# A transformer layer on one core: where the softmax sums are finished, in which order six and two merged tiles enter the output projection, and when LN1's statistics are called

## The chip, the cores and the metric

The kernel runs on one core of one Trainium2 chip. The metric is device time in microseconds of one execution; the median of several runs counts. An execution's span, from its first to its last instruction in the profile, is a little shorter than its device time.

Engines go by their short names: PE is TensorE, DVE VectorE, ACT ScalarE, POOL GpSimd, SP SyncE. Each engine takes its instructions in a fixed order and waits at one whose inputs are not ready or whose output buffer is still in use.

## What is computed

One layer of a diffusion backbone: 1024 latent tokens and 256 context tokens of width 1024. Two attention branches in parallel, A with a window of 128 to either side and a sink logit for each head, B over all keys; both also see the context keys. Eight heads each, 64 wide, two groups of keys and values. The branches are merged by sigmoid gates and projected; then come a residual with LayerNorm (LN1), a SwiGLU feed-forward with a convolution, and LN2. Cut to what matters here:

```python
def _sink_softmax(scores, sink):
    sink = sink.astype(jnp.float32)[:, :, None, None]
    m = jnp.maximum(jnp.max(scores, axis=-1, keepdims=True), sink)
    e = jnp.exp(scores - m)
    return e / (jnp.sum(e, axis=-1, keepdims=True) + jnp.exp(sink - m))

def _merge_branches(o_a, o_b, gate_logits, w_branch_a, w_branch_b, w_out):
    g_a, g_b = jnp.split(jax.nn.sigmoid(gate_logits), 2, axis=-1)
    return (g_a * (o_a @ w_branch_a) + g_b * (o_b @ w_branch_b)) @ w_out
...
        h = x * (1.0 + scale1) + shift1
        y = _latent_token_mixer(h, kv_ctx, w_in[l], b_in[l], attn_sink[l], q_norm_g[l], k_norm_g[l],
                                w_branch_a[l], w_branch_b[l], w_out[l], rope)
        x = _layer_norm(DEEPNORM_ALPHA * x + gate1 * y, ln1_g[l], ln1_b[l])

        h = x * (1.0 + scale2) + shift2
        y = _conv_ffn(h, w_up[l], conv_w[l], conv_b[l], w_down[l])
        x = _layer_norm(DEEPNORM_ALPHA * x + gate2 * y, ln2_g[l], ln2_b[l])
```

Branch B uses the ordinary softmax.

## The kernel before

All data are float32. For a product a value is split into a rounded high part and the rest (`split`, L86 the cast on ACT, L88 that on POOL, L91 the subtraction), and three matmuls make one product: high by high (L94), high by low (L95), low by high (L96), in `mm3`.

**Attention.** There are 32 units (class `Unit`, L421): branch A first, then B, eight blocks of 128 queries each, two groups of four heads each. The loop over u interleaves three lists by fractional positions: the score steps of unit u, the value steps of unit u-1, and other work that fills in (projections of the branches). Inside this stage a scheduler sets the order on every engine from the order in which the code issues and from its own estimates; the code's order is not the final one.

- Score steps: `context` (in B: four passes over the context keys, matmuls into `s_x`, then `cxp` at L515 on DVE, which writes `p_x`), four times `lat` (L466: matmuls L451/L452 into `s`, a pass on DVE at L497 that scales and finds the maximum, the exponential on ACT at L464 with the sum into `sm`, in B also the context's sum into `smc`), then `norm`, and the preparation of a later unit's queries (`qtr`).
- `norm` finishes the softmax sums of a unit. In A it adds the maximum and the sink (L522), takes the exponential on ACT (L523, tile `f`) and adds it to `sm` (L524); in B it adds `smc` to `sm` (L524). Then comes the reciprocal (L525). All of these are 128x4.
- Value steps: `tr_step` transposes four 128x128 pieces of probabilities on PE (L562) into `ptr`; ACT casts them to `pth` (L571) and DVE subtracts to get `ptl` (L572), or POOL does it for some key blocks; `av_step` multiplies by the values (L583 with `pth`, L584 with `ptl`). A step is one key block in A and two in B. `rows`, inserted as the third value step, transposes the reciprocal sums (L529, `str`), copies them and sends them through DRAM to all partitions (`rb`); the unit's last step, `out_step`, multiplies by `rb` on POOL (L598).
- `ptr`, `qtr` and `str` share three buffers in PSUM; `s` has two.

**Output projection.** `merge(f)` (L997) adds the two branches' gated results for the f-th of eight tiles (DVE, L999) and splits the sum into `mh` (ACT) and `ml` (DVE). `half(f, hf)` makes the product of branch B that `merge(f)` needs. `y_pair(f, s)` (L1252) makes the output tiles f and f+1 for the tokens in s: for each, eight merged tiles k by three matmuls of 128x512, with the weights `hwo` and `lwo`. From L1264 on the order of PE is the one written in the code.

**Planner.** `mm_ticked` (L1229) calls `tick` (L1086) after each k, which advances a counter by 640 for 512 columns. Steps in `pend` are issued when the counter reaches their number; the first step of LN1's first half (512 tokens) is `stats`, and its number is the first of `LN1_F` (L38), counted from the first k of `y_pair` over the second half's tokens. `stats` (L1106) issues 16 matmuls 128x1 (L1113 of `zs`, L1114 of `zq`) and a few small instructions on DVE and POOL; `diags` and `cast` (L1130) follow, then the tiles' normalization, which makes the operands of the up projection. `zs` and `zq` are the sums over tiles of the residual and of its square, added up on POOL (L1080) and DVE (L1081) as the tiles of `y` are done.

Of the kernel before, what the change touches and what calls it, by code (L numbers as in the profile page):

```python
# [9 lines left out]
AF = mybir.ActivationFunctionType  # L10
ALU = mybir.AluOpType
AX = mybir.AxisListType

P = 128
# [3 lines left out]
KT = 8  # L18
# [10 lines left out]
HALF = 512  # L29
# [5 lines left out]
FILL_END = 26  # L35
XPOS = 2
SPAN = 0.8, 0.85
LN1_F = 3500.0, 5100.0, 100.0  # L38
LN1_D = (2500.0, 2000.0, 2000.0, 2500.0), (300.0, 3700.0, 300.0, 500.0), (100.0, 1000.0, 300.0, 500.0)
LN2_D = 4000.0, 2800.0, 2000.0, 1200.0, 1300.0  # L40
LN2_E = 3500.0, 1500.0, 1500.0, 500.0, 400.0
# [30 lines left out]
def layer_kernel(  # L72
# [6 lines left out]
    nc = tc.nc  # L79
# [13 lines left out]
    def mm3(ps, a, b, start, stop, resumed=False):  # L93
        nc.tensor.matmul(ps, a[0], b[0], start=start, stop=False, skip_group_check=resumed)  # L94
        nc.tensor.matmul(ps, a[0], b[1], start=False, stop=False, skip_group_check=resumed)  # L95
        return nc.tensor.matmul(ps, a[1], b[0], start=False, stop=stop, skip_group_check=resumed).ins  # L96
# [12 lines left out]
    sinkb = ctile([P, 8], F32, "sinkb")  # L109
# [125 lines left out]
    for n in (0, 1):  # L235
        s = slice(n * HALF, (n + 1) * HALF)
# [10 lines left out]
    w = modulate(0)  # L247
    for k in range(KT):
# [5 lines left out]
        for t in range(NT):  # L254
            s = slice(t * P, (t + 1) * P)
            mm3(acc[t], (hT[k][0][:, s], hT[k][1][:, s]), w, k == 0, k == KT - 1)
        w = wn
# [163 lines left out]
    class Unit:  # L421
# [82 lines left out]
        def cxp(self):  # L504
# [7 lines left out]
            for h in range(4):  # L512
# [2 lines left out]
                nc.vector.tensor_scalar(out=p[:, c], in0=s[:, c], scalar1=self.qscale(nqs)[:, h:h + 1], scalar2=TOP,  # L515
                                        op0=ALU.mult, op1=ALU.min, accum_out=self.other[:, h:h + 1])

        def norm(self):
            hc = slice(self.g * 4, self.g * 4 + 4)
            more = self.smc if self.br else small(f"f_{self.id}", (P, 4))  # L520
            if not self.br:
                nc.vector.tensor_tensor(out=more, in0=self.nm, in1=sinkb[:, hc], op=ALU.add)  # L522
                nc.scalar.activation(more, more, AF.Exp)  # L523
            nc.vector.tensor_tensor(out=self.sm, in0=self.sm, in1=more, op=ALU.add)  # L524
            nc.vector.reciprocal(self.sm, self.sm)  # L525

        def rows(self):
# [11 lines left out]

        def score_steps(self):  # L540
            steps = [lambda h=h: self.lat(h) for h in range(4)]
            return steps + [self.norm]

        def context(self):
            self.begin()
# [8 lines left out]
        def value_steps(self):  # L554
# [57 lines left out]
            self.av_step, self.out_step = av_step, out_step  # L612
            g = 1 + self.br
            steps = [lambda n=n: step(range(n, n + g)) for n in range(0, len(kt), g)]
            steps.insert(2, self.rows)
            return steps

    tokens = []
# [125 lines left out]
    steps = [(gi, k, a) for gi, k in order for a in ((0, 1) if gi == "g" else (0,))]  # L744
# [15 lines left out]
    for n, (gi, k, a) in enumerate(steps):  # L760
# [17 lines left out]
        w = ready.pop((gi, k, 0))  # L778
        c = ready.pop(("c", k), None)
        for t in tiles:  # L780
            if t < NT:
                s = slice(t * P, (t + 1) * P)
                x = hT[k][0][:, s], hT[k][1][:, s]
            else:
                s = slice((t - NT) * P, (t - NT + 1) * P)
# [45 lines left out]
    def small(name, shape):  # L831
        return att.tile(list(shape), F32, tag=name.split("_")[0], name=name,
                        bufs=4)
# [58 lines left out]
    for u in range(nu + 1):  # L892
# [8 lines left out]
        if u == 29:  # L901
            first = branch_steps(1, w_b, (0, 1), att, (nc.gpsimd, nc.gpsimd), (0,),
                                 lambda: [ht(f"{a}wb1_0", (P, 8, P), R32) for a in "hl"])
# [74 lines left out]
    mrg = []  # L978
# [6 lines left out]
    wts = {}  # L985
# [45 lines left out]
    for f in range(2, KT):  # L1031
# [3 lines left out]
        ps = pb[f]  # L1035
# [190 lines left out]
        a, n = {"T3": ("13", 0), "T1": ("13", 1), "T4": ("24", 0), "T2": ("24", 1)}[name]  # L1226
        return tp[a + "h", k][:, n], tp[a + "l", k][:, n]

    def mm_ticked(o, w, a, s, n=KT):  # L1229
        for k in range(n):  # L1230
            mm3(o, (w[0][:, k], w[1][:, k]), (a[k][0][:, s], a[k][1][:, s]), k == 0, k == n - 1)
            tick((s.stop - s.start) / 0.8)

    npair = [0]
# [17 lines left out]
    def y_pair(f, s, first=False):  # L1252
        w = s.stop - s.start
        ps = big(f"y{f}_{s.start}_{w}")
        for a in (0, 1):
            mm_ticked(ps[:, a * HALF:a * HALF + w], wts[f + a], mrg, s)
        for a in (0, 1):
            wout_z(f + a, s, ps[:, a * HALF:a * HALF + w], first and a == 0)

# [14 lines left out]
    for f in (4, 6):  # L1274
        for si in (1, 2):
# [3 lines left out]
            elif f == 6:  # L1279
                second = ln1(2)  # L1280
                a = [n for n in range(len(pend)) if len(pend) - n <= KT]
# [122 lines left out]
    for k in range(4):  # L1404
        steps = build(k)
# [245 lines left out]
    s = LN2_S[-1]  # L1651
# [181 lines left out]
```

## Time and profile before

| | us |
|---|---|
| median of three runs | 1550.84 |
| the three runs | 1550.83, 1550.84, 1552.32 |
| the profiled execution | 1552.42 |
| its span | 1550.6 |
| PE busy | 1526.3 |
| DVE busy | 1164.9 |
| ACT busy | 802.1 |
| POOL busy | 753.1 |

The profile is of one execution, with a mean granted clock of 0.997. Matmuls overlap in it: the row of a matmul lasts longer than the step to the next one, so a stall of PE is read from start to start. In a row of the timeline stand start, duration, engine, line, operation, output and inputs, shapes, and in square brackets how long the engine was idle before it and what ended that. Attention lies between about 320 and 780 us, the output projection between 794 and about 890, the feed-forward behind it.

### The profile page before, as it was taken

To read this page: it belongs to the slowest core of one execution; us is meant where nothing else is said; L and a number is where in the kernel's file an instruction comes from. 1 tells how busy PE (TensorE), PEld (TensorE's weight loads), DVE (VectorE), ACT (ScalarE), POOL (GpSimd) and SP (SyncE) were. 2 spreads that over 40 slices of the span, in tenths; PEclk is the share of its full clock that TensorE was granted. 3 is DMA by queue.
4 is the path that set the end of the run, shared out by engine and by line. 5 is a ranking of instruction groups with operands and counts; after the bars stand their busy time and mean duration, and the time that the engine had idled before them with its cause. 6 is when DMAs were issued, how large, how long until landed. Compare 5 with 4: busy or idle time off the path is not lost. (4 is left out here: it accounts for less than half of the span.)

```text
span 1550.6 us, 21959 instructions
## 1 busy us (share of the span) xinstructions
PE 1526.3 (98%) x7652; PEld 1269.6 (82%) x7652; DVE 1164.9 (75%) x1783; ACT 802.1 (52%) x1420; POOL 753.1 (49%) x697
## 2 busy tenths in 40 slices
PE   9999999999999999999999999999999999999997
PEld 7888888878887788888778988888888888888886
DVE  7588847538888667788565879888888887657796
ACT  5422223448888666788422664544444444435542
POOL 0374303426666466565423555766666675021063
PEclk9999999999999999999999999999999999999999
DMA  9667663322236555543451223233334446996732
GB/s 379 244 214 260 234 227 91 112 88 63 63 106 163 133 120 130 116 93 86 161 146 59 82 82 109 95 111 114 115 109 105 113 109 174 368 276 214 256 113 91
DMA packets 111873, 229.73 MB, mean 148 GB/s; under 512 B 13489, under 2 KB 27313, under 8 KB 111666
## 3 DMA queue, kind: packets, MB, share of 16 engines
q1 hardware_dynamic: 96464, 199.20, 38.4%
q0 software_dynamic: 10400, 20.19, 8.5%
q10 hardware_dynamic: 4898, 8.94, 1.5%
q8 instruction: 60, 0.98, 0.3%
q14 instruction: 51, 0.42, 0.1%
HBM read 177.09 MB, written 65.87 MB: 157 GB/s over the span
## 5 line engine op out<-in xcount | busy, mean ns | idle before, releaser
L572 DVE TENSOR_TENSOR ptl<-ptr,pth 128x512 fp32r<-128x512 f32 x188 | 123.5, 685 | 32.6 <-ACT pth L571 31.8
L91 DVE TENSOR_TENSOR ld<-rd,hd 128x1024 fp32r<-128x1024 f32 x77 | 96.6, 1271 | 49.8 <-ACT hd L86 47.7
L562 PE MATMUL ptr<-ident,p 128*128 128x128 f32 x816 | 127.0, 277 | 5.5 <-DVE ptl L572 2.7
L571 ACT CAST pth<-ptr 128x512 fp32r<-128x512 f32 x188 | 105.5, 586 | 50.6 <-PE ptr L562 35.6
L464 ACT ACTIVATE p<-p,nm 128x1024 f32<-128x1024 f32 (+2 forms) x128 | 125.1, 979 | 10.5 <-DVE p L497 10.0
L86 ACT CAST hd<-rd 128x1024 fp32r<-128x1024 f32 x77 | 79.6, 1051 | 85.6 <-PE p L96 56.3
L562 PEld LDWEIGHTS ptr<-ident,p 128*128 128x128 f32 x816 | 95.1, 140 | 33.4 <-DVE ptl L572 7.7
L583 PE MATMUL av<-pth,VT 128*128 128x512 f32 x236 | 105.0, 445 | 1.2 <-ACT pth L571 0.9
L94 PE MATMUL p<-hd 128*128 128x512 f32 x264 | 103.2, 391 | 0.0
L96 PE MATMUL p<-hd,ld 128*128 128x512 f32 x264 | 102.7, 389 | 0.0
L95 PE MATMUL p<-ld,hd 128*128 128x512 f32 x264 | 102.7, 389 | 0.0
L96 PE MATMUL g<-hh,wlg 128*128 128x512 f32 x256 | 99.7, 390 | 0.4 <-POOL wlg L91 0.4
L94 PE MATMUL g<-hh,whg 128*128 128x512 f32 x256 | 99.9, 390 | 0.0
L95 PE MATMUL g<-hl,whg 128*128 128x512 f32 x256 | 99.6, 389 | 0.0
L584 PE MATMUL av<-ptl,VT 128*128 128x512 f32 x236 | 97.6, 414 | 0.5 <-POOL ptl L91 0.5
L91 POOL TENSOR_TENSOR wlg<-wg,whg 128x512 fp32r<-128x512 f32 x32 | 45.3, 1421 | 99.0 <-ACT whg L86 94.0
L497 DVE TENSOR_SCALAR_CACHE_REDUCE p<-s,cvt,nmc 128x1024 f32<-128x1024 f32 x64 | 84.6, 1339 | 7.4 <-PE ptr L562 5.5
L451 PE MATMUL s<-KL,q 128*128 128x512 f32 (+2 forms) x192 | 77.0, 401 | 1.3 <-DVE p_x L515 1.1
L88 POOL TENSOR_SCALAR pth<-prw 128x512 fp32r<-128x512 f32 x48 | 30.5, 635 | 93.4 <-PE av L583 43.9
L452 PE MATMUL s<-KL,q 128*128 128x512 f32 (+2 forms) x192 | 71.4, 372 | 0.0
L86 ACT CAST wS<-s 128x512 fp32r<-128x512 f32 x76 | 45.2, 620 | 49.7 <-POOL s L1166 48.9
L86 ACT CAST wA<-ru 128x512 fp32r<-128x512 f32 x57 | 35.5, 623 | 61.3 <-PE d L96 32.8
(403 smaller groups left out, 4918.4 us busy)
## 6 DMA issues: line engine op xcount, KB each, us to landing
wml<-in_wmodT_dram SPq DMA_DIRECT2D x48, 512.0 KB
ru<-in_w_up_dram SPq DMA_DIRECT2D x38, 512.0 KB
rd<-td SPq DMA_DIRECT2D x55, 256.0 KB
rd<-sd SPq DMA_DIRECT2D x44, 256.0 KB
rd<-in_w_dn_dram SPq DMA_DIRECT2D x33, 256.0 KB
wm<-in_wmodT_dram SPq DMA_DIRECT2D x16, 512.0 KB
wg<-in_w_g_dram SPq DMA_DIRECT2D x32, 256.0 KB
sgd<-sg ACTq DMA_DIRECT2D x32, 256.0 KB
```

The costliest lines, as they stand in the source:

```text
L86: cast[:] = [nc.scalar.copy(hi, src).ins]
L91: low[:] = [lo_eng.tensor_tensor(out=lo, in0=src, in1=hi.bitcast(F32), op=ALU.subtract).ins]
L94: nc.tensor.matmul(ps, a[0], b[0], start=start, stop=False, skip_group_check=resumed)
L95: nc.tensor.matmul(ps, a[0], b[1], start=False, stop=False, skip_group_check=resumed)
L96: return nc.tensor.matmul(ps, a[1], b[0], start=False, stop=stop, skip_group_check=resumed).ins
L464: nc.scalar.activation(p, s, AF.Exp, bias=nm[:, h:h + 1], scale=scale, accum_out=sm[:, h:h + 1])
L497: nc.vector.tensor_scalar(out=p, in0=o, scalar1=self.qscale(nqs)[:, hs] if self.br else -1.0, scalar2=self.other[:, hs], op0=ALU.mult, op1 ...
L562: nc.tensor.transpose(tr[:, h * P:(h + 1) * P], self.pslice(h, n), ident)
L571: nc.scalar.copy(hi, tr)
L572: nc.vector.tensor_tensor(out=lo, in0=tr, in1=hi.bitcast(F32), op=ALU.subtract)
L583: nc.tensor.matmul(self.av, v, hi, start=first, stop=False)
L584: nc.tensor.matmul(self.av, v, lo, start=False, stop=self.left == 0)
```

## The change

Three edits.

```diff
--- before.py
+++ after.py
@@ -35,7 +35,7 @@
 FILL_END = 26
 XPOS = 2
 SPAN = 0.8, 0.85
-LN1_F = 3500.0, 5100.0, 100.0
+LN1_F = 4500.0, 5100.0, 100.0
 LN1_D = (2500.0, 2000.0, 2000.0, 2500.0), (300.0, 3700.0, 300.0, 500.0), (100.0, 1000.0, 300.0, 500.0)
 LN2_D = 4000.0, 2800.0, 2000.0, 1200.0, 1300.0
 LN2_E = 3500.0, 1500.0, 1500.0, 500.0, 400.0
@@ -515,13 +515,13 @@
                 nc.vector.tensor_scalar(out=p[:, c], in0=s[:, c], scalar1=self.qscale(nqs)[:, h:h + 1], scalar2=TOP,
                                         op0=ALU.mult, op1=ALU.min, accum_out=self.other[:, h:h + 1])
 
+        def sink(self):
+            self.smc = small(f"f_{self.id}", (P, 4))
+            nc.vector.tensor_tensor(out=self.smc, in0=self.nm, in1=sinkb[:, self.g * 4:self.g * 4 + 4], op=ALU.add)
+            nc.scalar.activation(self.smc, self.smc, AF.Exp)
+
         def norm(self):
-            hc = slice(self.g * 4, self.g * 4 + 4)
-            more = self.smc if self.br else small(f"f_{self.id}", (P, 4))
-            if not self.br:
-                nc.vector.tensor_tensor(out=more, in0=self.nm, in1=sinkb[:, hc], op=ALU.add)
-                nc.scalar.activation(more, more, AF.Exp)
-            nc.vector.tensor_tensor(out=self.sm, in0=self.sm, in1=more, op=ALU.add)
+            nc.vector.tensor_tensor(out=self.sm, in0=self.sm, in1=self.smc, op=ALU.add)
             nc.vector.reciprocal(self.sm, self.sm)
 
         def rows(self):
@@ -539,7 +539,7 @@
 
         def score_steps(self):
             steps = [lambda h=h: self.lat(h) for h in range(4)]
-            return steps + [self.norm]
+            return steps if self.br else steps + [self.sink]
 
         def context(self):
             self.begin()
@@ -612,7 +612,8 @@
             self.av_step, self.out_step = av_step, out_step
             g = 1 + self.br
             steps = [lambda n=n: step(range(n, n + g)) for n in range(0, len(kt), g)]
-            steps.insert(2, self.rows)
+            steps[2:2] = [self.rows]
+            steps[1:1] = [self.norm]
             return steps
 
     tokens = []
@@ -1226,9 +1227,9 @@
         a, n = {"T3": ("13", 0), "T1": ("13", 1), "T4": ("24", 0), "T2": ("24", 1)}[name]
         return tp[a + "h", k][:, n], tp[a + "l", k][:, n]
 
-    def mm_ticked(o, w, a, s, n=KT):
-        for k in range(n):
-            mm3(o, (w[0][:, k], w[1][:, k]), (a[k][0][:, s], a[k][1][:, s]), k == 0, k == n - 1)
+    def mm_ticked(o, w, a, s, ks):
+        for k in ks:
+            mm3(o, (w[0][:, k], w[1][:, k]), (a[k][0][:, s], a[k][1][:, s]), k == 0, k == KT - 1)
             tick((s.stop - s.start) / 0.8)
 
     npair = [0]
@@ -1252,8 +1253,9 @@
     def y_pair(f, s, first=False):
         w = s.stop - s.start
         ps = big(f"y{f}_{s.start}_{w}")
-        for a in (0, 1):
-            mm_ticked(ps[:, a * HALF:a * HALF + w], wts[f + a], mrg, s)
+        for ks in (range(6), range(6, KT)) if first and s.start == 0 else (range(KT),):
+            for a in (0, 1):
+                mm_ticked(ps[:, a * HALF:a * HALF + w], wts[f + a], mrg, s, ks)
         for a in (0, 1):
             wout_z(f + a, s, ps[:, a * HALF:a * HALF + w], first and a == 0)
```

**Softmax sums.** `norm` is cut in two. The sink's part, an add on DVE and the exponential on ACT, stays among the score steps of branch A, as `sink`; B has one score step fewer, so the others move in their fractional positions. The add to `sm` and the reciprocal become the second of the unit's value steps, which run in the next iteration: first transposes, `norm`, second transposes, `rows`, and so on. No instruction is added or removed.

**Output projection.** The first `y_pair` (tiles 0 and 1, first half of the tokens) takes k from 0 to 5 for tile 0, then for tile 1, then k 6 and 7 for tile 0 and for tile 1. The other pairs are as before. `tick` is called as often.

**Statistics.** The first number of `LN1_F` goes from 3500 to 4500: with 640 for each k, `stats` is issued after the eighth k instead of the sixth, so after 24 matmuls of 128x512 instead of 18. What follows counts from there.

The following rows show the instructions in an engine's order. A name ends in a number of the buffer, which differs between the two kernels and means nothing.

PE at the beginning of the output projection, before (`y0_0_512` is the pair's result; `mh5`, `ml5` the sixth merged tile, `hwo0`, `lwo0` the weights of output tile 0):

```order
L96 MATMUL y0_0_512_8997<-mh5_8866,lwo0_8873 128x512
L94 MATMUL y0_0_512_8997<-mh6_8911,hwo0_8872 128x512
L95 MATMUL y0_0_512_8997<-ml6_8912,hwo0_8872 128x512
L96 MATMUL y0_0_512_8997<-mh6_8911,lwo0_8873 128x512
L94 MATMUL y0_0_512_8997<-mh7_8944,hwo0_8872 128x512
L95 MATMUL y0_0_512_8997<-ml7_8945,hwo0_8872 128x512
L96 MATMUL y0_0_512_8997<-mh7_8944,lwo0_8873 128x512
L94 MATMUL y0_0_512_8997<-mh0_8753,hwo1_8950 128x512
```

and now:

```order
L96 MATMUL y0_0_512_8997<-mh5_8866,lwo0_8873 128x512
L94 MATMUL y0_0_512_8997<-mh0_8753,hwo1_8950 128x512
L95 MATMUL y0_0_512_8997<-ml0_8754,hwo1_8950 128x512
L96 MATMUL y0_0_512_8997<-mh0_8753,lwo1_8951 128x512
...
L96 MATMUL y0_0_512_8997<-mh5_8866,lwo1_8951 128x512
L94 MATMUL y0_0_512_8997<-mh6_8911,hwo0_8872 128x512
L95 MATMUL y0_0_512_8997<-ml6_8912,hwo0_8872 128x512
L96 MATMUL y0_0_512_8997<-mh6_8911,lwo0_8873 128x512
L94 MATMUL y0_0_512_8997<-mh7_8944,hwo0_8872 128x512
```

The sixth merged tile is followed by the first merged tile with the second output tile's weights; mh6 and mh7 come 18 matmuls later.

DVE in branch B between the units 1_1_1 and 1_2_0, before (`ptl1_1_0_7` is the copy for key block 7 of unit 1_1_0; `sm`, `smc` the sums, `p1_2_0_x` the context passes):

```order
L572 TENSOR_TENSOR ptl1_1_0_5_5778<-ptr1_1_0_5_5772,pth1_1_0_5_5777 128x512
L497 TENSOR_SCALAR p1_1_1_2_5735,nm_1_1_1_5609<-s1_1_1_2_5730,cvt_69,nmc_1_1_1_5620 128x1024
L497 TENSOR_SCALAR p1_1_1_3_5759,nm_1_1_1_5609<-s1_1_1_3_5754,cvt_69,nmc_1_1_1_5620 128x1024
L515 TENSOR_SCALAR p1_2_0_x_5863,nmc_1_2_0_5861<-s1_2_0_x_5852,cvt_69 128x256 x3
L524 TENSOR_TENSOR sm_1_1_1_5610<-sm_1_1_1_5610,smc_1_1_1_5621 128x4
L515 TENSOR_SCALAR p1_2_0_x_5863,nmc_1_2_0_5861<-s1_2_0_x_5852,cvt_69 128x256
L525 RECIPROCAL sm_1_1_1_5610<-sm_1_1_1_5610 128x4
L572 TENSOR_TENSOR ptl1_1_0_7_5802<-ptr1_1_0_7_5796,pth1_1_0_7_5801 128x512
L497 TENSOR_SCALAR p1_2_0_0_5913,nm_1_2_0_5850<-s1_2_0_0_5908,cvt_69,nmc_1_2_0_5861 128x1024
```

and now:

```order
L572 TENSOR_TENSOR ptl1_1_0_5_5778<-ptr1_1_0_5_5772,pth1_1_0_5_5777 128x512
L497 TENSOR_SCALAR p1_1_1_2_5727,nm_1_1_1_5607<-s1_1_1_2_5722,cvt_69,nmc_1_1_1_5618 128x1024
L497 TENSOR_SCALAR p1_1_1_3_5759,nm_1_1_1_5607<-s1_1_1_3_5754,cvt_69,nmc_1_1_1_5618 128x1024
L572 TENSOR_TENSOR ptl1_1_0_7_5813<-ptr1_1_0_7_5807,pth1_1_0_7_5812 128x512
L515 TENSOR_SCALAR p1_2_0_x_5861,nmc_1_2_0_5859<-s1_2_0_x_5850,cvt_69 128x256 x4
L572 TENSOR_TENSOR ptl1_1_0_8_5834<-ptr1_1_0_8_5828,pth1_1_0_8_5833 128x512
L572 TENSOR_TENSOR ptl1_1_0_9_5843<-ptr1_1_0_9_5837,pth1_1_0_9_5842 128x512
L572 TENSOR_TENSOR ptl1_1_1_0_5872<-ptr1_1_1_0_5866,pth1_1_1_0_5871 128x512
L572 TENSOR_TENSOR ptl1_1_1_1_5881<-ptr1_1_1_1_5875,pth1_1_1_1_5880 128x512
L497 TENSOR_SCALAR p1_2_0_0_5911,nm_1_2_0_5848<-s1_2_0_0_5906,cvt_69,nmc_1_2_0_5859 128x1024
L524 TENSOR_TENSOR sm_1_1_1_5608<-sm_1_1_1_5608,smc_1_1_1_5619 128x4
L525 RECIPROCAL sm_1_1_1_5608<-sm_1_1_1_5608 128x4
```

The add and the reciprocal of unit 1_1_1 stood around the last context pass of unit 1_2_0; now the four passes are together, and the add and the reciprocal come behind two copies of unit 1_1_1's own value steps and behind the first latent pass of unit 1_2_0.

DVE at the last unit, 1_7_1, before:

```order
L497 TENSOR_SCALAR p1_7_1_3_8431,nm_1_7_1_8294<-s1_7_1_3_8426,cvt_69,nmc_1_7_1_8305 128x1024
L572 TENSOR_TENSOR ptl1_7_0_7_8452<-ptr1_7_0_7_8446,pth1_7_0_7_8451 128x512
L572 TENSOR_TENSOR ptl1_7_0_8_8469<-ptr1_7_0_8_8463,pth1_7_0_8_8468 128x512
L524 TENSOR_TENSOR sm_1_7_1_8295<-sm_1_7_1_8295,smc_1_7_1_8306 128x4
L525 RECIPROCAL sm_1_7_1_8295<-sm_1_7_1_8295 128x4
L572 TENSOR_TENSOR ptl1_7_0_9_8478<-ptr1_7_0_9_8472,pth1_7_0_9_8477 128x512
```

and now:

```order
L497 TENSOR_SCALAR p1_7_1_3_8431,nm_1_7_1_8316<-s1_7_1_3_8426,cvt_69,nmc_1_7_1_8327 128x1024
L572 TENSOR_TENSOR ptl1_7_0_7_8452<-ptr1_7_0_7_8446,pth1_7_0_7_8451 128x512
L524 TENSOR_TENSOR sm_1_7_1_8317<-sm_1_7_1_8317,smc_1_7_1_8328 128x4
L525 RECIPROCAL sm_1_7_1_8317<-sm_1_7_1_8317 128x4
L572 TENSOR_TENSOR ptl1_7_0_8_8467<-ptr1_7_0_8_8461,pth1_7_0_8_8466 128x512
L572 TENSOR_TENSOR ptl1_7_0_9_8476<-ptr1_7_0_9_8470,pth1_7_0_9_8475 128x512
```

The last latent pass and the copy for key block 7 of unit 1_7_0 come first as before; the add and the reciprocal of unit 1_7_1 now stand ahead of the copy for key block 8 instead of behind it.

## The prediction

> **What bounds the kernel now.** I read the first part of the page, then the waits of TensorE, then stretches of the timeline around each place that the change touches.
>
> ```profile
> PE 1526.3 (98%) x7652; PEld 1269.6 (82%) x7652; DVE 1164.9 (75%) x1783; ACT 802.1 (52%) x1420; POOL 753.1 (49%) x697
> ```
>
> TensorE is busy for 1526.3 of 1550.6 us, and the change keeps its arithmetic. So only time in which TensorE stands still, or runs below its full clock, can be won. Its waits, one row for each reason (total, times, longest, in us):
>
> ```profile
> PE ptr L562 <- DVE ptl L572: 2.7, 3, 1.5
> ...
> PE y L94 <- ACT mh L86: 1.1, 1, 1.1
> ...
> PE s L451 <- DVE p_x L515: 1.1, 1, 1.1
> ...
> PE y L95 <- DVE ml L91: 0.8, 1, 0.8
> ...
> PE sta L1114 <- DVE zq L1081: 0.2, 1, 0.2
> ```
>
> The two `y` rows are the seventh merged tile, the `sta` row is the statistics of LN1: two parts of the change are aimed at them. The other two rows stand in the attention stage, where the third part works. None is large, so neither is the prize.
>
> **Output projection.** The start of `y` (start, duration, engine, line, operation):
>
> ```profile
> 794.21 0.39 PE L94 MATMUL y<-mh,hwo 128*128 128x512 f32 x1
> ...
> 798.74 0.39 PE L96 MATMUL y<-mh,lwo 128*128 128x512 f32 x1
> ...
> 799.17 1.04 ACT L86 CAST mh<-bT 128x1024 fp32r<-128x1024 f32 x1 [4.15 <-DVE bT L999]
> ...
> 800.25 1.23 DVE L91 TENSOR_TENSOR ml<-bT,mh 128x1024 fp32r<-128x1024 f32 x1 [1.11 <-ACT mh L86]
> ...
> 800.27 0.50 PE L94 MATMUL y<-mh,hwo 128*128 128x512 f32 x1 [1.14 <-ACT mh L86]
> ...
> 801.53 0.50 PE L95 MATMUL y<-ml,hwo 128*128 128x512 f32 x1 [0.76 <-DVE ml L91]
> ```
>
> From 794.21 to 798.74 TensorE starts 21 matmuls (seven merged tiles by three), so 20 steps take 4.53 us and one takes 0.2265, although each row lasts 0.39: matmuls overlap, and a stall is read from start to start. The matmul on mh7 was due at 798.74 + 0.23 = 798.97 and starts at 800.27: 1.30 late. The one on ml7 was due 0.23 later and starts after 1.26: another 1.03. Sum 2.33 us.
>
> After the change 36 matmuls (six tiles for each of the two output tiles) and the three on mh6 stand ahead of mh7: it is due at 794.21 + 39 x 0.2265 = 803.04, ml7 at 803.27. The rows have them finished at 799.17 + 1.04 = 800.21 and 800.25 + 1.23 = 801.48. The wait is gone with 1.8 us to spare. What is late next? The second tile's weights are wanted sooner, at 794.21 + 18 x 0.2265 = 798.29, and the next pair's at 794.21 + 48 x 0.2265 = 805.08:
>
> ```profile
> 783.21 1.63 DVE L91 TENSOR_TENSOR lwo<-rwo,hwo 128x1024 fp32r<-128x1024 f32 x1
> ...
> 802.50 1.05 ACT L86 CAST hwo<-rwo 128x1024 fp32r<-128x1024 f32 x1 [2.28 <-DMA rwo<-in_w_out_dram]
> ...
> 803.58 2.49 DVE L91 TENSOR_TENSOR lwo<-rwo,hwo 128x1024 fp32r<-128x1024 f32 x2 [2.11 <-ACT hwo L86]
> ```
>
> The second tile's low part is done at 784.84. The next pair's high part is there at 803.55, its low part at 803.58 + 1.25 = 804.83, wanted by the third matmul at 805.53: 0.7 us to spare. No new wait, and no DMA is issued elsewhere. **Term: -2.3** (bounds -2.3 and -1.6, the latter if the next pair's low part came 1.4 us later, twice its spare).
>
> **Statistics of LN1.** The first number of LN1_F makes the 16 small matmuls come after 24 matmuls of the next pair instead of 18.
>
> ```profile
> 841.33 3.00 POOL L1080 TENSOR_TENSOR zs<-zs,z 128x512 f32<-128x512 f32 x2 [7.88 <-DVE z L1152]
> ...
> 841.95 2.93 DVE L1081 TENSOR_TENSOR zq<-zq,sqa 128x512 f32<-128x512 f32 x2
> ...
> 844.38 0.38 PE L1113 MATMUL sta<-onec,zs 128*128 128x1 f32 x2
> 844.93 0.38 PE L1114 MATMUL sta<-onec,zq 128*128 128x1 f32 x2 [0.17 <-DVE zq L1081]
> ...
> 846.51 0.48 PE L94 MATMUL y<-mh,hwo 128*128 128x512 f32 x1
> ...
> 851.16 0.40 PE L95 MATMUL y<-ml,hwo 128*128 128x512 f32 x1
> ```
>
> The sums are complete at 844.33 (POOL) and 844.88 (VectorE). The last 14 small matmuls take 846.51 - 844.93 = 1.58 us, 0.113 each, so all 16 need 1.81; they take 846.51 - 844.38 = 2.13. The wait is 0.3 us. Six matmuls (1.36 us) later the first is due at about 845.7, behind both sums: **term -0.3** (bounds 0 and -0.4).
>
> Behind it the clock falls. Windows (stretch, length, busy times of the five engines, granted clock, DMA share, GB/s):
>
> ```profile
> 847.00:851.00 4.00, 4.00 (x12) 3.09 (x12) 1.59 (x5) 0.00 (x0) 1.03 (x1) 0.58 0.00 0
> ...
> 1485.00:1490.00 5.00, 5.00 (x32) 4.43 (x31) 4.32 (x7) 1.06 (x2) 0.53 (x1) 1.00 0.53 162
> ```
>
> In the first row the granted clock is 0.58. From 846.51 to 851.16 TensorE takes 13 steps, which at 0.2265 would need 2.94 and need 4.65: 1.7 us lost. In the second row the same 16 small matmuls of LN2 run without a wait, and the clock stays at 1.00. One case with a wait and a fall, one without either: I take it that the fall goes with the wait. **Term -1.7** (bounds 0 and -1.7).
>
> [...]
>
> Since the statistics come 1.36 us later, so do the normalized tiles; their consumer, the up projection, stands behind at least 72 more matmuls of `y`, 16 us by the step above. Nothing for that, at most +1.4 (the shift itself) if the second half's statistics were pushed by all of it.
>
> **Softmax sums.** An add and a reciprocal for each of 32 units move behind the first transposes' copies of the following iteration; the number of instructions and of DMAs stays. What they hold up today is VectorE (waits of VectorE, 320 to 760 us, and the source line's summary, ns):
>
> ```profile
> DVE sm L524 <- ACT f L523: 11.2, 12, 1.1
> ...
> DVE sm L524 <- ACT p_x L464: 2.4, 4, 0.9
> ```
>
> ```profile
> L524 DVE TENSOR_TENSOR sm<-sm,smc x16: 152/162/1594, 474.8 to 739.2; 128x4 f32<-128x4 f32 x16
> ```
>
> So VectorE stands still for 13.6 us, in front of an add that usually needs 0.16. But the windows say how little of it TensorE feels:
>
> ```profile
> 320.00:380.00 60.00, 55.39 (x350) 47.37 (x349) 39.66 (x91) 40.72 (x97) 27.42 (x37) 1.00 0.28 84
> 380.00:440.00 60.00, 59.91 (x397) 50.94 (x396) 52.34 (x124) 51.79 (x123) 39.53 (x59) 1.00 0.25 66
> ...
> 560.00:680.00 120.00, 119.95 (x702) 99.61 (x701) 87.76 (x179) 89.34 (x197) 78.42 (x95) 1.00 0.54 123
> ```
>
> In the steady stretches of both branches (second and third row) TensorE misses 0.09 of 60 and 0.05 of 120 us, while VectorE waited in front of most of these adds: **term 0 there**. Gain and loss can come only at the transients. One is clear:
>
> ```profile
> 529.65 1.59 DVE L524 TENSOR_TENSOR sm<-sm,smc 128x4 f32<-128x4 f32 x1
> ...
> 530.14 0.49 PE L583 MATMUL av<-pth,VT 128*128 128x512 f32 x1 [0.86 <-ACT pth L571]
> 530.26 0.96 POOL L91 TENSOR_TENSOR qs<-Q,qs 128x256 fp32r<-128x256 f32 x1
> ...
> 531.17 0.47 DVE L515 TENSOR_SCALAR_CACHE_REDUCE p_x<-s_x,cvt 128x256 f32<-128x256 f32 x1
> ...
> 531.70 0.50 PE L451 MATMUL s<-KL,q 128*128 128x512 f32 x1 [1.07 <-DVE p_x L515]
> ```
>
> Here the four-column add took 1.59 us, ending with a POOL instruction (530.26 + 0.96 = 531.22). It stood ahead of the last context pass of unit 1_2_0, and TensorE waited 1.07 us for that pass. In the new order the four passes stand together with no add between them: **term -1.1** (bounds 0 and -1.3).
>
> [...]
>
> The other clear one is a loss. At the end of the last unit:
>
> ```profile
> 736.93 1.32 DVE L572 TENSOR_TENSOR ptl<-ptr,pth 128x512 fp32r<-128x512 f32 x2
> ...
> 739.20 0.16 DVE L524 TENSOR_TENSOR sm<-sm,smc 128x4 f32<-128x4 f32 x1 [0.94 <-ACT p_x L464]
> ...
> 739.39 0.18 DVE L525 RECIPROCAL sm<-sm 128x4 f32<-128x4 f32 x1
> ```
>
> Two copies ran ahead of the add, which waited for the last exponential. In the new order the add and the reciprocal stand between these copies: the second copy, done at 738.25 before, cannot end before 739.20 + 0.16 + 0.18 + 0.66 = 740.2, 2 us later. Behind it wait the second product of that key block and the third transpose group after it, since three buffers are shared. I take half of it as cost, **+1.0** (bounds 0 and +2.0).
>
> At the start of the stage the order changes too, and there a stall can move either way:
>
> ```profile
> 342.73 2.28 DVE L522 TENSOR_TENSOR f<-nm,sinkb 128x4 f32<-128x4 f32 x1
> ...
> 345.67 0.66 PE L562 MATMUL ptr<-ident,p 128*128 128x128 f32 x4 [1.47 <-DVE ptl L572]
> ```
>
> A stretched sink add delayed a copy, and TensorE waited 1.47. The sink add now stands one copy earlier. I take 0 (bounds -1.5 and +1.5).
>
> **Sum:** -2.3 - 0.3 - 1.7 - 1.1 + 1.0 = -4.4 us. The profiled execution took 1552.42 with a span of 1550.6 (1.8 around it), 1.6 above the median, like the highest of the three runs; since the terms are differences, they are set against the median: 1550.84 - 4.4 = **1546.4**.
>
> **Rivals.**
>
> R1, no help in the attention: the wait at 531.70 only passes to the next late copy (four copies now stand ahead of pass 1_2_0_0 on VectorE) and the 1.47 of 345.67 comes a second time: 1546.4 + 1.1 + 1.5 = **1549.0**. For it: TensorE missed nothing in the steady stretches. Against it: the add at 529.65 plainly ended last there.
>
> R2, the relief of VectorE reaches TensorE at the start of branch A, where TensorE misses 60.00 - 55.39 = 4.6 us: 1546.4 - 4.6 = **1541.8**. For it: the row of 2.7 us on `ptl` and the 11.2 us of idle VectorE. Against: part of the 4.6 waits for exponentials.
>
> R3, slower: in branch B the add waits for the last exponential of its unit in front of the copies, as worked out for the last unit, in each of 15 units. A wait of 0.94 each, passed on to TensorE, is 14.1 us, with the 4.3 of the later stages 1550.84 - 4.3 + 14.1 = 1560.6; half of it gives 1553.6. About **1557**. It decides from 0.5 us per unit on, where (3.1 + 4.3) / 15 is passed. For it: a TensorE without reserve (119.95 of 120). Against: VectorE is idle for 32 of these 120 us, and the waits for `f` of today, 11.2 / 12 = 0.9 each, cost TensorE nothing in the second window.
>
> R4, the clock falls all the same after the moved statistics: 1546.4 + 1.7 = **1548.1**. [...]
>
> **How the numbers follow.** Two runs of this kernel are told apart from about 0.2% on, 3.1 us: faster is below 1547.7, slower above 1553.9. Forecast 0.46, its own range 1544 to 1549 by the bounds of the clock term, the tail and the start of the stage; 0.37 of it is faster, 0.09 within. R2 0.20, faster. R4 0.08, of which 0.07 within. R1 0.11, within. R3 0.15, slower. Faster 0.58, same 0.27, slower 0.15. The range of 8 in 10 runs from 1540 (R2 with a little more) to 1554; above it lies R3.
>
> **What would show it.** Right, if the rows `y <- mh`, `y <- ml` and `sta <- zq` are missing from TensorE's waits, with the granted clock at 1.00 in the 10 us behind the statistics; if 529 to 532 us has no wait for `p_x`; if around 738 TensorE waits about 1 us longer. Wrong, if the attention stage from 320 to 780 us is longer or shorter by more than 2 us: then the moved sums decide and not the later stages.

## The result, and the profile after

The changed kernel takes 1569.0 us (median, 1567.7 to 1570.4) against 1550.9 before: ratio 1.0115, 95% interval 1.0097 to 1.0132. It is 18 us slower, above the predicted range. The profiled execution has a span of 1568.5 us, 17.9 more than before. Behind the edits the line numbers are one or two higher.

The first part of the page, after:

```profile
PE 1528.9 (97%) x7652; PEld 1271.5 (81%) x7652; DVE 1170.0 (75%) x1783; ACT 801.4 (51%) x1420; POOL 753.9 (48%) x697
```

The work is the same; TensorE stands still longer. Its waits after (total, times, longest, us):

```profile
PE av L584 <- POOL ptl L91: 7.3, 10, 0.9
PE av L583 <- ACT avs L589: 3.8, 6, 1.6
PE s L451 <- DVE p L497: 3.0, 3, 1.3
PE ptr L562 <- ACT rb L532: 2.4, 1, 2.4
...
PE av L583 <- POOL pth L88: 1.7, 2, 1.1
```

None of these five rows stands in the list of before with more than 0.5 us. All are in the attention; `rb` is the copy of the transposed sums that `rows` makes. The rows `y <- mh`, `y <- ml`, `sta <- zq` and `s <- p_x` of before are gone. The windows of the two steady stretches after:

```profile
380.00:440.00 60.00, 55.11 (x366) 47.99 (x364) 47.08 (x111) 46.43 (x110) 36.21 (x53) 1.00 0.22 54
560.00:680.00 120.00, 114.49 (x648) 94.33 (x647) 78.84 (x163) 78.23 (x172) 68.41 (x82) 0.99 0.53 119
```

TensorE now misses 4.9 of 60 and 5.5 of 120 us, where it missed 0.09 and 0.05. VectorE is less busy, not more: it is not the bound. In the second stretch the granted clock is 0.99 and not 1.00, because it falls there once:

```profile
624.00:628.00 4.00, 2.08 (x5) 1.47 (x6) 2.41 (x7) 1.29 (x3) 3.44 (x4) 0.76 0.04 13
628.00:632.00 4.00, 4.00 (x18) 3.21 (x17) 1.16 (x2) 0.59 (x1) 0.00 (x0) 0.82 1.01 144
```

The fall lasts 3.41 us at a granted clock of 0.50 (the clock record of this profile), from 626.05, between two waits of TensorE for POOL's split (1.10 us until 625.07, 0.85 us until 626.43).

Where the time goes is read from the copy of each unit's finished value product (`avs`, one for each unit). First before, then after: a row for the steady stretch of branch A and one from the sixteenth unit, the last of A, to the end (count, shortest/median/longest ns, first and last start).

```profile
L589 ACT COPY avs<-av x8: 592/593/595, 383.9 to 442.4; 128x512 f32<-128x512 f32 x8
...
L589 ACT COPY avs<-av x17: 568/592/597, 478.7 to 752.2; 128x512 f32<-128x512 f32 x17
```

```profile
L589 ACT COPY avs<-av x7: 573/576/586, 384.2 to 439.6; 128x512 f32<-128x512 f32 x7
...
L589 ACT COPY avs<-av x17: 567/590/602, 485.7 to 773.5; 128x512 f32<-128x512 f32 x17
```

A unit of branch A takes 58.5 / 7 = 8.36 us before and 55.4 / 6 = 9.23 after. Branch A ends 485.7 - 478.7 = 7.0 us later, branch B takes 287.8 instead of 273.5, another 14.3. Everything behind it, 17.9 - 21.3, gains 3.4. In branch B (after: 485 to 774 us, before: 478 to 752) TensorE's waits sum to 14.5 us, before to 3.3. No one wait leads: the largest rows are 3.8 us for `avs`, whose copy frees the buffer of the next unit's product, and 2.4 us for `rb`. With the 1.7 us that the fall of the clock cost in the profile before, that is 12.9 of the 14.3.

The later stages went nearly as the sum had them. The merge and the statistics after:

```profile
815.51 0.39 PE L94 MATMUL y<-mh,hwo 128*128 128x512 f32 x1
...
821.89 1.23 DVE L91 TENSOR_TENSOR ml<-bT,mh 128x1024 fp32r<-128x1024 f32 x1 [1.12 <-ACT mh L86]
...
824.35 0.39 PE L94 MATMUL y<-mh,hwo 128*128 128x512 f32 x1
...
827.21 0.50 PE L96 MATMUL y<-mh,lwo 128*128 128x512 f32 x1 [0.20 <-DVE lwo L91]
...
864.97 0.28 PE L1114 MATMUL sta<-onec,zs 128*128 128x1 f32 x2
```

```profile
864.00:868.00 4.00, 4.00 (x27) 3.58 (x27) 0.66 (x4) 0.00 (x0) 0.45 (x1) 1.00 0.00 0
868.00:872.00 4.00, 4.00 (x18) 3.12 (x17) 1.36 (x3) 0.00 (x0) 0.58 (x1) 1.00 0.02 4
```

The matmul on mh7 comes 8.84 us after the first (39 steps of 0.2265 are 8.83), ml7 has been ready since 823.12, and neither is waited for. One short wait is new: the next pair's low weights (827.21), which the sum had with 0.7 us to spare, come late and cost 0.4 us from start to start (827.21 - 826.61 - 0.23). The statistics start without a wait, and the granted clock stays at 1.00.

### The profile page after: what moved, and what is told of

It is laid out like the page before. It is cut to its first block, busy times and chain, and to the rows that moved or that the text cites. A ratio compares the mean times of both kernels' runs of the same rounds, so it can differ in the third digit from the quotient of the medians.

```text
span 1568.5 us, 21978 instructions
## 1 busy us (share of the span) xinstructions
PE 1528.9 (97%) x7652; PEld 1271.5 (81%) x7652; DVE 1170.0 (75%) x1783; ACT 801.4 (51%) x1420; POOL 753.9 (48%) x697
## 5 line engine op out<-in xcount | busy, mean ns | idle before, releaser
L562 PE MATMUL ptr<-ident,p 128*128 128x128 f32 x816 | 120.6, 276 | 5.3 <-ACT rb L532 2.4
```

The costliest lines, as they stand in the source:

```text
L562: nc.tensor.transpose(tr[:, h * P:(h + 1) * P], self.pslice(h, n), ident)
```

## The experiments

Each is compared with the kernel before on the same chip; there its median was 1551.5 to 1551.8 us. A ratio stands with its 95% interval. The kernels are built on different bases: those with the sums behind the second transposes, with `PLAG`, with `POOL_LO` and under "What is better than both" hold the two later edits, which are worth 2.9 us by the first experiment; the other attention kernels do not.

**Which part.** The two later edits alone, and the moved sums alone (`LN1_F` at 3500, `mm_ticked` and `y_pair` as before).

> The kernel before with the two later edits alone: six merged tiles first, and statistics after 24 matmuls. The attention is that of before. Both theories agree here: the waits on mh7, ml7 and zq and the clock fall behind the statistics go, 4.3 us in all, so 1550.9 - 4.3 = 1546.6 us, and between 780 and 860 us of the profile TensorE has no wait above 0.3 us. If the change had lost something behind the attention as well, it would come out above 1548.

Measured: 1548.80 us, ratio 0.9979 (0.9969 to 0.9988). No row of `y` or `sta` is left among the waits. The gain is 2.9 us, 4.3 is inside the interval (1.9 to 4.8).

> The change without its two later edits: only the softmax sums are moved. If the whole loss lies in the attention and the later edits gain what the sum gave them, 1569.0 + 4.3 = 1573.3 us. If the later edits share in the loss, at or below 1569.

Measured: 1573.58 us, ratio 1.0135 (1.0120 to 1.0150). The whole loss lies in the edit of the softmax sums.

**The moved instructions, or the moved positions.** Theory S blames the shifted positions, theory D the moved instructions; they are separated by doing the one without the other. First the sums are moved and the positions kept (against the changed kernel, without its later edits):

```diff
-            return steps if self.br else steps + [self.sink]
+            return steps + [(lambda: None) if self.br else self.sink]
...
-            steps[2:2] = [self.rows]
-            steps[1:1] = [self.norm]
+            first_ = steps[0]
+            def opening():
+                first_()
+                self.norm()
+            steps[0] = opening
+            steps.insert(2, self.rows)
```

> Only the softmax sums are moved, behind the same transposes as in the change, but without a place of their own: the add and the reciprocal are called at the end of the first value step, and branch B keeps an empty score step, so every other step keeps the position that it has before. Theory S (the new value step and the missing score step shift the positions of the other steps, and TensorE gets another order): no loss, 1549 to 1552 us. Theory D (the add and the reciprocal stand in the way of VectorE's copies, the third rival of the prediction): most of the loss stays, 1565 to 1573 us.

Measured: 1550.15 us, ratio 0.9991 (0.9981 to 1.0000). Then the positions are shifted and the sums left (against the kernel before):

```diff
-            return steps + [self.norm]
+            if not self.br:
+                return steps + [self.norm]
+            def last():
+                self.lat(3)
+                self.norm()
+            return steps[:3] + [last]
...
-            steps.insert(2, self.rows)
+            steps[2:2] = [self.rows]
+            steps[1:1] = [lambda: None]
```

> The sums stay where they are before, at the end of the score steps (in branch B inside the last latent step), but the value steps get an empty step in second place and branch B has one score step fewer: the positions of the change without the move of any instruction. Theory S: the loss is here, 1568 to 1576 us. Theory D: about the time of before, 1549 to 1553 us.

Measured: 1569.91 us, ratio 1.0112 (1.0097 to 1.0127), with no sum moved behind anything. As the cause of the loss theory D is out: finishing the sums behind the first transposes costs nothing where the positions are kept. An empty entry in the value list and one entry fewer in branch B's score list cost 18 us. The moved sums are not quite free beside them: the edit as a whole took 1573.58 us, another 3.7.

**Which of the two lists.** Each half of the last diff alone.

> Only the empty step in second place of the value steps; the score steps of branch B and the place of the sums are those of before. Theory V (the later value steps, pushed back by one place in seven, lose the time alone): 1566 to 1573 us, with the waits of the value product for POOL's copy in branch A as in the change. Theory B (the missing score step of branch B is needed for the loss there): branch A loses its 7 us, branch B little, 1556 to 1560 us.

> Only the score step of branch B is missing (the sums are called inside the last latent step); the value steps are those of before. Theory V: 1549 to 1554 us. Theory B: 1558 to 1565 us, with the loss between 470 and 780 us of the profile.

Measured: 1564.70 us, ratio 1.0084 (1.0070 to 1.0097) for the value list, 1552.13, ratio 1.0000 (0.9991 to 1.0010), for the score list. The value list does most of it. The time lies below the first forecast and above the second; the shorter score list adds some 5 us only beside the longer value list. By the rows of `avs`, branch A ends at 486.2 us with the longer value list alone, at 486.2 with both lists changed and at 486.0 with the sums moved too: its 7 us are the value list's. Branch B takes 278.3, 283.2 and 287.9 us (before: 273.5), so its loss comes in three parts of nearly 5 us. These are single profiles; two of the three hold a fall of the clock in B, worth up to 1.7 us.

**Which step.** With seven value steps in place of six (five key-block steps, rows, sums), the second transposes go from 1.5 / 6 = 0.25 to 2.5 / 7 = 0.357 of the iteration. In branch A the second latent step stands at 0.8 x 2.5 / 7 = 0.286 (the score steps fill the first 0.8 of the iteration), between them. In the first try the sums stand behind the second transposes, which brings these back to 1.5 / 7 = 0.214:

```diff
-            steps[2:2] = [self.rows]
-            steps[1:1] = [self.norm]
+            steps[2:2] = [self.norm, self.rows]
```

> The whole change, but the sums are finished behind the second transposes instead of the first: the value list has the same length, with second transposes, sums, rows in this order. The second transposes then come ahead of the second latent step again, as before the change, while the rows stay late. Theory C (the loss comes from the second transposes falling behind the second latent step): branch A is back at 8.36 us per unit from 9.25, and the time comes to 1546 to 1552 us. If it is the longer list as such, or the late rows, that costs: 1562 us or more.

Measured: 1561.10 us, ratio 1.0065 (1.0044 to 1.0086). In the second the kernel before gets nothing but a later place for the second transposes:

```diff
+            steps[1].later = 0.06
             steps.insert(2, self.rows)
...
-                seq.append((of + sp * (n + 0.5) / len(lst), st_))
+                seq.append((of + sp * (n + 0.5) / len(lst) + getattr(st_, "later", 0.0), st_))
```

> The kernel before with nothing moved but the second transposes of every unit, set back by 0.06 of the iteration, just behind the second latent step. Theory C: branch A takes 9.2 to 9.3 us per unit and the whole 1558 to 1566 us. If the place of the second transposes alone is not the cause, 1550 to 1553 us.

Measured: 1565.11 us, ratio 1.0088 (1.0072 to 1.0104). The copies `avs`, first with the sums behind the second transposes, then with nothing but the second transposes set back:

```profile
L589 ACT COPY avs<-av x8: 592/592/594, 384.9 to 443.4; 128x512 f32<-128x512 f32 x8
...
L589 ACT COPY avs<-av x17: 568/592/606, 479.3 to 765.2; 128x512 f32<-128x512 f32 x17
```

```profile
L589 ACT COPY avs<-av x7: 572/576/585, 385.4 to 440.7; 128x512 f32<-128x512 f32 x7
...
L589 ACT COPY avs<-av x17: 564/572/596, 486.8 to 765.8; 128x512 f32<-128x512 f32 x17
```

For branch A this settles it: 58.5 / 7 = 8.36 us with the second transposes ahead of the second latent step in a list of seven, 55.3 / 6 = 9.22 with them behind it in a list of six. For the whole the forecast of the first kernel was wrong: its branch A ends at 479.3 as before, but branch B takes 285.9 in place of 273.5. In the second, B takes 765.8 - 486.8 = 279.0: there the second latent step stands at 0.85 x 2.5 / 7 = 0.304, and the second transposes, at 0.31, fall behind it too.

**Why 9.23 us in branch A.** One period of POOL and its neighbours, after (timeline, rows of four engines; `prw` is the raw copy of the key block that POOL splits, `up` and `ot` are tiles of `out_step`):

```profile
400.27 0.50 PE L584 MATMUL av<-ptl,VT 128*128 128x512 f32 x1 [0.75 <-POOL ptl L91]
...
402.60 0.58 ACT L589 COPY avs<-av 128x512 f32<-128x512 f32 x1
...
404.09 0.62 POOL L591 TENSOR_SCALAR up<-avs 64x512 f32<-64x512 f32 x1
...
404.74 0.85 DVE L595 TENSOR_TENSOR ot<-avs,up 64x256 f32<-64x256 f32 x2 [0.72 <-POOL up L591]
...
405.27 0.60 ACT L568 COPY prw<-ptr 128x512 f32<-128x512 f32 x1
...
405.73 0.74 POOL L598 TENSOR_TENSOR ot<-ot,rb 128x256 f32<-128x256 f32 x1 [1.02 <-DVE ot L595]
...
406.92 0.62 POOL L88 TENSOR_SCALAR pth<-prw 128x512 fp32r<-128x512 f32 x1
...
408.20 1.29 POOL L91 TENSOR_TENSOR ptl<-prw,pth 128x512 fp32r<-128x512 f32 x1
...
409.54 0.50 PE L584 MATMUL av<-ptl,VT 128*128 128x512 f32 x1 [0.77 <-POOL ptl L91]
```

and before:

```profile
400.65 0.59 ACT L589 COPY avs<-av 128x512 f32<-128x512 f32 x1
...
401.42 0.62 POOL L591 TENSOR_SCALAR up<-avs 64x512 f32<-64x512 f32 x1
...
403.23 0.60 ACT L568 COPY prw<-ptr 128x512 f32<-128x512 f32 x1
...
405.19 1.28 POOL L91 TENSOR_TENSOR ptl<-prw,pth 128x512 fp32r<-128x512 f32 x1
...
407.45 0.40 PE L584 MATMUL av<-ptl,VT 128*128 128x512 f32 x1
```

After, a ring can be read: the product on POOL's key block waits for POOL (400.27); the unit's last product and its copy `avs` follow; `up`, `ot` and the multiplication by `rb` use it one after the other; POOL does these ahead of the next unit's split, whose end at 409.49 releases the next such product at 409.54. Once around is 9.27 us, the period. Not every link is a dependency: `avs` also follows an exponential on ACT, and `up` the split of a later unit's queries on POOL; these are the engines' own orders. Before, the split ended at 406.47 and was wanted at 407.45: 1.0 us to spare, and TensorE's own work set the period (it missed 0.09 of 60 us). Two tries on that ring:

```diff
-PLAG = 1, 2
+PLAG = 2, 2
```

> The change with one number more: in branch A the value product of the key block that POOL splits is issued one transposing step later (first number of PLAG 2 in place of 1). If branch A loses because that product now comes too soon after its transposes, the eight waits of 0.7 us for POOL between 380 and 460 us go, and the time falls by 5 to 8 us, to 1561 to 1564 us. If the loss in branch A has another cause that only shows at this place, the wait passes to another copy and the time stays within 2 us of 1569.

Measured: 1575.67 us, ratio 1.0154 (1.0140 to 1.0168): worse. The waits for POOL between 380 and 460 us are gone, and this row has come:

```profile
PE str L529 <- DVE ptl L572: 6.6, 8, 1.0
```

Giving that product more time only hands the wait on. So it is not the distance of one product from its transposes.

```diff
-POOL_LO = (3,), (2, 6)
+POOL_LO = (), (2, 6)
```

> The change, with POOL's share of the copies in branch A given to VectorE (first entry of POOL_LO empty). Theory ring: a unit of branch A takes 9.25 us because POOL splits the fourth key block only behind the output step of the unit before, and that waits for the value products behind the one that waits for POOL. Without it the ring is open: 8.3 to 8.7 us per unit, VectorE being busy for about 8.0 of it, and the whole 1562 to 1565 us. If POOL only shows the wait, 9.0 us per unit or more and 1568 us or above.

Measured: 1562.60 us, ratio 1.0074 (1.0057 to 1.0090), and in branch A:

```profile
L589 ACT COPY avs<-av x8: 566/571/572, 381.8 to 439.3; 128x512 f32<-128x512 f32 x8
```

57.5 / 7 = 8.21 us per unit (the forecast was 8.3 to 8.7): with POOL's share taken out, branch A is even a little faster than before. This edit changes the order on other engines too, so it shows that the ring goes with POOL's share, not each of its links.

**Branch B.** Three kernels for what is left there: the sums behind the second transposes (as in the third diff) with an empty score step in B (as in the first); the sums called at the end of the second value step, without a place of their own; and an empty value step behind the second transposes with the sums where they were.

> The change with the sums behind the second transposes (as norm2, 1561.1 us) and an empty score step in branch B, so that the score steps keep their positions. If branch B needs the missing score step for its loss, 1547 to 1551 us. If the longer value list alone does it, 1557 to 1561 us.

> Only the sums are moved, to the end of the second value step, without a place of their own; all other steps keep the positions of the kernel before. If late sums are what branch B cannot bear: 1558 to 1563 us, with the loss between 480 and 765 us. If not: 1549 to 1553 us.

> The sums stay where they are before; the value list gets an empty step behind the second transposes, so that it is one longer but the second transposes stay ahead of the second latent step. If the longer list alone costs branch B its time: 1557 to 1562 us. If the list and the late sums are needed together: 1550 to 1553 us.

Measured: 1559.73 us, ratio 1.0054 (1.0039 to 1.0069); 1553.68 us, ratio 1.0020 (1.0010 to 1.0029); 1563.99 us, ratio 1.0081 (1.0064 to 1.0098). The first holds the later edits, so its attention loses some 11 us. The late sums without a place of their own cost some 2 us; the longer list alone costs 12, with the second transposes ahead of the second latent step all the time. In the last of the three, in an execution of 1566.97 us, the slowest of its four (rows of `avs`):

```profile
L589 ACT COPY avs<-av x8: 589/591/592, 384.1 to 442.6; 128x512 f32<-128x512 f32 x8
...
L589 ACT COPY avs<-av x17: 567/587/594, 484.4 to 765.8; 128x512 f32<-128x512 f32 x17
```

Branch A is at 8.36, the passage from A to B is 5.7 us late (484.4 against 478.7), and B takes 7.9 more than before. Most of the late passage can be read in its trace:

```profile
479.32 1.17 POOL L633 DMA_DIRECT2D sd<-in_w_dn_dram  x1 [8.61 <-DMA sd<-in_w_dn_dram]
...
481.20 0.50 PE L583 MATMUL av<-pth,VT 128*128 128x512 f32 x1 [3.10 <-POOL pth L88]
...
483.47 0.80 PE L584 MATMUL av<-ptl,VT 128*128 128x512 f32 x1 [1.77 <-POOL ptl L91]
```

POOL stands for 8.61 us in front of the issue of a DMA (a sum of feed-forward weights) that waits for the one before it, and TensorE then waits 4.9 us for the split behind it. Before, POOL stood 2.4 us there (473.40) and TensorE waited 0.5. So a part of this kernel's 12 us comes from the order in which POOL issues its DMAs. Reckoned as above, the one exchange between score and value steps in most of B is `rows` (from 0.417 to 0.5), which falls behind the third latent step (0.425); whether this or an exchange with the filling work costs B its 7.9 us was not tried, and two falls of the clock lie in this profile (483.34 and 643.77).

**The two later edits apart.**

> The kernel before with only the six merged tiles first. By the terms of the prediction the two waits of 1.1 and 0.8 us on the seventh merged tile go, -2.3 us, and the wait on the statistics stays at 0.2 to 0.3 us; where the clock falls once behind one of these waits today, it can still fall behind the statistics. 1551.8 - 2.3 = 1549.5 us.

> The kernel before with only the statistics called after 24 matmuls. By the terms the wait on the statistics goes, -0.3 us, and the fall of the clock behind it, -1.7 us: 1549.8 us. [...]

Measured: 1549.73 us, ratio 0.9988 (0.9975 to 1.0000), and 1549.24 us, ratio 0.9989 (0.9979 to 0.9999). Each gain is barely clear of nothing. In the first the wait on the statistics is left, and so is the fall of the clock behind it:

```profile
840.00:844.00 4.00, 3.83 (x26) 3.17 (x25) 2.01 (x5) 0.00 (x0) 1.23 (x1) 1.00 0.00 0
844.00:848.00 4.00, 4.00 (x12) 3.13 (x11) 1.52 (x4) 0.00 (x0) 1.03 (x1) 0.57 0.00 0
```

In the second the waits on mh7 and ml7 are left (0.6 and 0.8 us) and the clock does not fall: it stands at 1.00 in every window of 4 us from 780 to 1040.

**What is better than both.** The later edits with the sums moved and the old positions kept, and the same with POOL's share in A given to VectorE.

> The two later edits, and the softmax sums moved without a place of their own, as in the second experiment kernel. If the parts add up, 1550.15 - 1551.68 = -1.5 for the moved sums and 1548.80 - 1551.68 = -2.9 for the later edits give 1551.7 - 4.4 = 1547.3 us. If the gain of the moved sums was only noise of the runs, 1548.8 us.

> The two later edits, the sums moved without a place of their own, and POOL's share in branch A given to VectorE. With 8.2 instead of 8.36 us per unit over some 12 units of branch A, 2 us less than the 1546.1 us of the version without the last edit: 1544 us. If VectorE, now the busier, holds up TensorE at the change from branch A to B, 1546 us or more.

Measured: 1546.14 us, ratio 0.9967 (0.9955 to 0.9980), and 1546.12 us, ratio 0.9969 (0.9958 to 0.9980). The parts add up in the first. The second is no faster, against the forecast of 1544 us, although its branch A ends 6.4 us earlier (473.0 against 479.4): in its profile B gives back 2.2 us and the rest 2.3, at a mean granted clock of 0.997 against 0.999 in the first's.

## Why the prediction was wrong

The sign that the prediction named for being wrong, an attention stage longer by more than 2 us, came: it is 21 us longer. **The step that failed** is the sentence "term 0 there" on the steady stretches. It priced the moved add and reciprocal and nothing else; the text on the change says that the score steps of B move in their fractional positions, does not say that the value steps of both branches do, and the sum has no term for either. One entry more in a list of six puts every later step elsewhere. In branch A that costs 7 us, by the second transposes and the ring through POOL. Branch B loses 14, by the longer value list, the shorter score list and the moved sums together; which exchange of steps does it there stays open. That TensorE missed only 0.09 of 60 us was taken to mean that "gain and loss can come only at the transients". It says only that nothing is to be won: the spare of 1.0 us on POOL's split stood in the trace and did not enter the sum.

In effect the sum forecast another kernel: the one that moves the sums, keeps the positions and has the later edits measured 1546.14 us, 5.1 us less by its ratio (3.1 to 7.0), where the sum had 4.4 less.

**The third rival** had the sign, and at 1557 us not the size, and its mechanism does not make the loss: the sums behind the first transposes alone gave a ratio of 0.9991. Only beside the shifted positions do the moved sums cost 3.7 us.

**The merge** (-2.3): the mechanism was right. Both waits are gone, mh7 comes after 39 steps as worked out, and the edit alone gives 1549.73 - 1551.58 = -1.9 us (by its interval between -3.9 and 0). In the changed kernel 0.4 us of it goes to the wait for the low weights, inside the term's bounds.

**Statistics and clock** (-0.3 and -1.7): the edit alone gives 1549.24 - 1551.58 = -2.3 us (by its interval between -3.3 and -0.2), in sum with the merge -4.2 where -4.3 was forecast; the two together gave -2.9 with an interval that holds it. The reason "the fall goes with the wait" was too simple. Of 11 profiles (that of before among them) with a wait at the merge or at the statistics, 9 have a fall of the clock behind one of them, at either place, once at both; of 8 without these waits none has one there. So the fall goes with the waits, but they do not fix its place, and one may pass without it: with the statistics alone moved, waits of 0.6 and 0.8 us at the merge have the granted clock at 1.00 behind them. What picks among the waits no run shows. The times between the changes of the clock have a measure in common: in the clock records of the profiles before and after, each stretch from one change to the next is a whole multiple of 3.4133 us, the fall itself being one such step, 3.413 (before: 836.27 = 245 x 3.4133 up to the fall, 692.91 = 203 x 3.4133 behind it; after: 614.40 = 180 x and 931.84 = 273 x 3.4133). The fourth rival, a fall behind the moved statistics all the same, did not come: the granted clock was 1.00 there.

**The wait at 531.70** (-1.1): the row `s <- p_x` is gone, but other waits of B cover what it gave. Where the sums moved and the positions stayed, it is gone too, and B took 271.8 us in place of 273.5: the term holds there.

**The tail** (+1.0): there the add now waits 1.68 us for the last exponential, and two waits follow, in the profile after:

```profile
759.61 0.16 DVE L524 TENSOR_TENSOR sm<-sm,smc 128x4 f32<-128x4 f32 x1 [1.68 <-ACT p_x L464]
...
760.10 0.50 PE L583 MATMUL av<-pth,VT 128*128 128x512 f32 x1 [0.63 <-ACT pth L571]
...
760.83 0.66 PE L562 MATMUL ptr<-ident,p 128*128 128x128 f32 x4 [0.22 <-DVE ptl L572]
```

That is 0.85 us of waits near that place. Only the second, 0.22 us, hangs on VectorE's copy; the first waits for a cast on ACT, which follows the last exponential. Before, TensorE waited 0.51 us there (737.68). So the net is some 0.3 us: inside the bounds, but the size of 1.0 is not confirmed.

## What to carry to other kernels

Where the order of work comes from positions in lists, adding or taking out an entry is not free even if it is empty (18 us here): compare the order of the busiest engine as a whole before pricing the instruction that was moved, and give a new step a place inside an old one. A stage in which the bound engine has no idle time can still lose (here it missed 0.09 of 60 us before and 4.9 after). Follow each helper engine once around a period and note by how much its result is ahead of its use; where that spare is 1 us, as here, a shift by one step can close a ring that then sets the period (8.36 us before, 9.23 after).

## What was not expected of the hardware

The granted clock fell to 0.50 for 3.41 us (clock records before and after; in the windows of the other profiles some 3.4) after short waits of TensorE, of 0.2 us at the statistics or of 0.8 to 1.5 us at the merge, in 9 of 11 profiles, at one place or the other from kernel to kernel. In at least 7 of the 19 profiles it also fell in the attention: in that of the changed kernel behind a wait of 1.10 us, and in that of the empty value step behind the second transposes, at 483.34 us, behind one of 3.10. In the records before and after, the times from one of its changes to the next are whole multiples of 3.4133 us. One such fall cost 1.7 us in the profile before, beside 2.6 us for the waits at the merge and the statistics. Whether it is behind the differences of 1.5 to 3 us between executions of one kernel was not tried.
